# State-space mixer of a hybrid decoder layer: state products after all within-chunk products, the mask as an f32r product, transposes behind the f32r products

## The chip, the cores and the metric

The kernel runs on one core of a Trainium2 chip. The metric is the device time of one execution in microseconds, the median over repeated runs. A profile of one execution stands beside it; its times are microseconds from the first instruction unless marked ns.

## The reference, cut to what matters

One layer over 512 tokens: a normalisation, one input projection, two token mixers (a gated linear attention and a state-space mixer), one output projection, then a retrieval feed-forward over 16,384 experts and a last normalisation. The change lies in the state-space mixer, which works in four chunks of 128 tokens, with 8 heads of width 64 in 2 groups:

```python
seg = a_cum[:, :, :, None] - a_cum[:, :, None]
Lmat = jnp.exp(jnp.where(causal, seg, -jnp.inf))
Xdt = X * dt[..., None]
scores = jnp.einsum('bclgn,bcsgn->bclsg', Cm, Bm)
y_diag = jnp.einsum('bclsg,bclsgj,bcsgjp->bclgjp', scores, Lmat, Xdt)
decay_to_end = jnp.exp(a_cum[:, :, -1:] - a_cum)
states = jnp.einsum('bclgn,bclgj,bclgjp->bcgjpn', Bm, decay_to_end, Xdt)
...
y_off = jnp.einsum('bclgn,bcgjpn,bclgj->bclgjp', Cm, S_prev, jnp.exp(a_cum))
y = y_diag + y_off + X * d_skip.astype(f32).reshape(G, J)[..., None]
```

`y_diag` is the within-chunk product of a head, `y_off` its state product with the state that the earlier chunks left; the first chunk has no state.

## The kernel before

The order of work is written out by hand: each engine runs its instructions in the order in which the program issues them, and semaphores tie the engines together. One chunk `t` of the state-space mixer is three functions.

`ssd_a(t)` prepares. TensorE transposes the four blocks of X (L563, into `px`). For each of the two groups it forms the decay exponents of four heads with one f32r product each, whose operands have 40 rows (L569), adds the causal mask to all four with one product of a bf16 identity with a bf16 mask, 512 columns wide (L571), and ScalarE takes eight exponentials into `lm`. Four more f32r products with 40 rows give the decay for the state products (L578, into `ce` by VectorE). In chunks 0 to 2 one more transpose (L594) follows, then two f32 products with 64 rows, the scores (L601), which VectorE multiplies into `lm`. VectorE also scales X into `xdt` and `xdw`.

`ssd_b(t)` has, for each of the 8 heads, the within-chunk product (L614: 128 rows by 64 output partitions) and, from chunk 1 on, the state product added to it in the same PSUM region (L616: 64 rows by 64 output partitions; the row half is the group's, the output half is the head's parity). Then come the two products for the next state (L620). VectorE adds the skip term, gates, and with ScalarE's square makes `ysq`.

`ssd_c(t)` takes the group means (L647), an inverse root on ScalarE and VectorE, and splits the result into two f32r parts.

An f32 product is two instructions on TensorE, an f32r product is one. Between these functions the program places the output projection, `op(t, half, cols)`: twelve f32r products of 512 columns for each half of a token tile and of the columns (L108, L109, L110), and the residual and second normalisation (`hout_a`, `hout_b`, `n2out`; the transposes of the last are L716). PSUM has eight banks, handed out by `pt()` in turn as tiles are given back; a new tile waits for the last reader of the bank that it gets.

Of the kernel before, what the change touches and what calls it, by code (L numbers as in the profile page):

```python
# [8 lines left out]
F32R = mybir.dt.float32r  # L9
F16 = mybir.dt.float16  # L10
BF = mybir.dt.bfloat16
# [18 lines left out]
def bc(ap, axis, n):  # L30
    shape = list(ap.shape)
    shape.insert(axis, n)
    ix = tuple([slice(None)] * axis + [None])
    return ap[ix].to_broadcast(shape)
# [29 lines left out]
class Layer:  # L64
# [25 lines left out]
    def act(self, out, in_, f, **k):  # L90
        return self.S.activation(out, in_, f, **k)  # L91
# [4 lines left out]
    def tt(self, out, x, y, op):  # L96
        return self.V.tensor_tensor(out, x, y, op=op)  # L97

    def stt(self, out, x, s, y, op0, op1, **k):
        return self.V.scalar_tensor_tensor(out, x, s, y, op0=op0, op1=op1, **k)  # L100
# [31 lines left out]
    def mixers(self):  # L132
        tc, nc, a, V, T, ps = self.tc, self.nc, self.a, self.V, self.T, self.ps
        act, tt, stt, load = self.act, self.tt, self.stt, self.load
        ctx = ExitStack()
        c = ctx.enter_context(tc.tile_pool(name="mx", bufs=1))
        cr_ctx = ExitStack()
        cr = cr_ctx.enter_context(tc.tile_pool(name="mxr", bufs=1, side="right"))
        ident = self.ident

        def pt(shape=(128, 512)):
            return ps.tile(list(shape), F32, name="pm", tag="pm", bufs=8)

        def b4(dt=F32, shape=(128, 1024)):
            return c.tile(list(shape), dt, name="b4", tag="b4", bufs=29)

        def tp(shape=(128, L)):
            return cr.tile(list(shape), F32, name="tp", tag="tp", bufs=11)
# [9 lines left out]
        def ahead(i, nl=None, ns=None):  # L158
            nl, ns = look if nl is None else (nl, ns)
            while seen[0] <= min(i + nl, len(blocks) - 1):  # L160
                j = seen[0]
                raws[j] = cr.tile([128, 1024], F32, name="wraw", tag="wraw", bufs=3)
                load(raws[j], blocks[j])
                seen[0] += 1
            while seen[1] <= min(i + ns, len(blocks) - 1):
                j = seen[1]
                parts[j] = b4(F32R), b4(F32R)
                self.split(parts[j][0], parts[j][1], raws.pop(j), j < 2 or 19 <= j < 31)
                seen[1] += 1
# [93 lines left out]
        px = [pt() for _ in range(8)]  # L263
# [3 lines left out]
        for dc in range(8):  # L267
# [3 lines left out]
            stt(nl[dc], px[dc], wmix[:, dc:dc + 1], nh[dc].bitcast(F32), OP.mult, OP.subtract)  # L271
            if dc == 4:
                ahead(0, 3, 1)
        negm = c.tile([128, 128], BF, name="negm")
        identb = c.tile([128, 128], BF, name="identb")
        V.tensor_copy(negm, negm0)
        V.tensor_copy(identb, ident)

        selE, selH = c.tile([40, 4, 128], F32R, name="selE"), c.tile([40, 8], F32R, name="selH")
        V.memset(selE.bitcast(F32)[0:32], 0.0)  # L280
# [198 lines left out]
        SG, SZ, XB = [], [], {}  # L479
# [78 lines left out]

        def ssd_a(t):
            ts = slice(t * 128, (t + 1) * 128)  # L560
            px = pt()
            for b in range(4):
                T.transpose(px[:, b * 128:(b + 1) * 128], XB[b][:, ts], ident)  # L563
            lm = b4(F32, (128, 8, 128))
            for g in range(2):
                p = pt()
                for j in range(4):
                    h = 4 * g + j
                    T.matmul(p[:, j * 128:(j + 1) * 128], selH[:, h:h + 1].to_broadcast([40, 128]), acs[:, ts],  # L569
                             start=j == 0, stop=False, skip_group_check=True)  # L570
                T.matmul(p, identb, bc(negm, 1, 4), start=False, stop=True, skip_group_check=True)  # L571
                for j in range(4):
                    h = 4 * g + j
                    act(lm[:, h, :], p[:, j * 128:(j + 1) * 128], AF.Exp, bias=nacT(t)[:, h:h + 1])
            LM[t] = lm
            p = pt()
            for j in range(4):
                T.matmul(p[:, j * 128:(j + 1) * 128], selE[:, j, :], eas[:, ts], start=True, stop=True)  # L578
            ce = tp((128, 4, 128))
            p3 = p.rearrange("p (j l) -> p j l", j=4)  # L580
            tt(ce, p3, bc(XB[5][:, ts], 1, 4), OP.mult)
            de = c.tile([128, 4], F32, name="de", bufs=2)
            V.tensor_copy(de, p3[:, :, 127])
            CE[t], DEC[t] = ce, de
            px3 = px.rearrange("p (h n) -> p h n", h=8)
            xdt, xdw = tp((128, 8, 64)), None
            tt(xdt, px3, bc(dtT(t), 2, 64), OP.mult)
            if t < NT - 1:
                xdw = tp((128, 8, 64))
                tt(xdw, px3, bc(dwT(t), 2, 64), OP.mult)  # L590
            pb = None
            if t < NT - 1:
                pb = pt()
                T.transpose(pb[:, :128], XB[4][:, ts], ident)  # L594
                bt = c.tile([128, 128], F32, name="bt", bufs=2)
                act(bt, pb[:, :128], AF.Copy)
                pb = bt
            psc = [pt(), pt()]
            for g in range(2):
                r = slice(g * 64, g * 64 + 64)  # L600
                T.matmul(psc[g][:, :128], XB[4][r, ts], XB[5][r, ts], start=True, stop=True)  # L601
                tt(lm[:, 4 * g:4 * g + 4, :], lm[:, 4 * g:4 * g + 4, :], bc(psc[g][:, :128], 1, 4), OP.mult)
            XT[t] = xdt, xdw, pb

        def ssd_b(t):
            ts = slice(t * 128, (t + 1) * 128)
            xdt, xdw, bt = XT.pop(t)
            lm, ce, S = LM.pop(t), CE.pop(t), Sd[t]
            py = [pt(), pt()]
            for h in range(8):  # L610
                g, j = h // 4, h % 4
                r = slice(g * 64, g * 64 + 64)
                o = py[g][(j % 2) * 64:(j % 2) * 64 + 64, (j // 2) * 128:(j // 2) * 128 + 128]
                T.matmul(o, xdt[:, h, :], lm[:, h, :], start=True, stop=S is None)  # L614
                if S is not None:
                    T.matmul(o, S[r, j, :], ce[r, j, :], start=False, stop=True)  # L616
            if t < NT - 1:
                pst = pt()
                for g in range(2):
                    T.matmul(pst[g * 64:g * 64 + 64, :256], bt[:, g * 64:g * 64 + 64], xdw[:, 4 * g:4 * g + 4, :],  # L620
                             start=True, stop=True)
                pst3 = pst[:, :256].rearrange("p (j n) -> p j n", j=4)
                Sn = c.tile([128, 4, 64], F32, name="Sd", bufs=2)
                if S is None:
                    act(Sn, pst3, AF.Copy)
                else:
                    tt(Sn, S, bc(DEC[t], 2, 64), OP.mult)
                    tt(Sn, Sn, pst3, OP.add)
                Sd[t + 1] = Sn
            y = tp((128, 4, 128))  # L630
            for b in range(4):
                stt(y[:, b, :], XB[b][:, ts], dsk[:, b:b + 1], py[b // 2][:, (b % 2) * 128:(b % 2) * 128 + 128],
                    OP.mult, OP.add)
            for b in range(2):
                tt(y[:, 2 * b:2 * b + 2, :], y[:, 2 * b:2 * b + 2, :], sz_[b][:, :, ts], OP.mult)
            ysq = tp((128, 4, 128))
            act(ysq, y, AF.Square)
            tt(ysq[:, 0:4:2, :], ysq[:, 0:4:2, :], ysq[:, 1:4:2, :], OP.add)
            yy[t] = y, ysq
# [123 lines left out]
        flush()  # L763
        self.table("natural_log_exp_and_others")
        ssd_a(0)
        op(1,0,(1,))
        ssd_b(0)
        ssd_a(1)
        ssd_c(0)
        wo(4)  # L770
        op(0,0,(0,))
        xload(2)
        ssd_b(1)
        op(0,1,(0,))
        xload(1)
        xload(0)
        op(0,1,(1,))
        hout_a(0)
        ssd_a(2)
        hout_b(0)  # L780
        ssd_c(1)
        op(2,0,(1,))
        ssd_b(2)
        n2out(0)
        op(1,1,(0,))
# [681 lines left out]
```

## Time and profile before

| | us |
|---|---|
| median of 3 runs (lowest, highest) | 1524.52 (1524.38, 1526.88) |
| profiled execution, its own time | 1525.01 |
| its span, first to last instruction | 1523.2 |
| TensorE busy in the span | 1479.2 |
| VectorE busy | 1168.4 |
| ScalarE busy | 632.3 |
| GpSimd busy | 451.6 |

The profile is one execution. The span is 1.8 us shorter than that execution's own time, and that execution is 0.5 us above the median. The state-space chunks lie between 171.4 and 243 us of the span. Busy time counts a matmul until its modelled end, and matmuls overlap, so the distance between two starts tells more of a product's cost than its duration.

### The profile page before, as it was taken

The numbers are of one execution on the slowest core, as the hardware profiler recorded it, in microseconds if no ns is written. First come the engines' busy times: TensorE is split into PE (matmuls) and PEld (weight loads), VectorE is DVE, ScalarE is ACT, GpSimd is POOL, SyncE is SP. The second block draws the span as 40 slices with busy tenths as digits, with TensorE's granted clock in tenths as the row PEclk, the third lists the DMA queues.
The fourth block names the chain that finished last, engine by engine and source line by source line (L and its number), as shares of the span: only waits on it lengthen the run. The fifth ranks groups of instructions, "written<-read, shape, count | busy, mean of one in ns | idle before, by whom it ended". The sixth has DMA issues, their size and how long they took to land.

```text
span 1523.2 us, 22401 instructions
## 1 busy us (share of the span) xinstructions
PE 1479.2 (97%) x7904; PEld 1290.1 (85%) x7904; DVE 1168.4 (77%) x2473; ACT 632.3 (42%) x1201; POOL 451.6 (30%) x380
## 2 busy tenths in 40 slices
PE   7999999999988999989999999999999999999997
PEld 6777767888988999878999999999889998888886
DVE  6543654599999999977777777787788788888886
ACT  5335633433653544433333333333333333444444
POOL 1002403444564000002333333333243333334332
PEclk9999999999999999999999999999999999999999
DMA  5231213322334556658889888889889897888894
GB/s 186 83 125 56 70 53 131 108 84 90 105 110 140 157 150 169 180 180 301 317 304 322 317 307 303 318 309 316 297 317 316 314 322 257 293 301 301 298 327 178
DMA packets 148738, 335.56 MB, mean 220 GB/s; under 512 B 64640, under 2 KB 73872, under 8 KB 148496
## 3 DMA queue, kind: packets, MB, share of 16 engines
q1 hardware_dynamic: 58672, 186.32, 36.0%
q0 software_dynamic: 36864, 134.23, 24.6%
q10 hardware_dynamic: 53088, 13.57, 3.8%
q8 instruction: 62, 1.02, 0.3%
q14 instruction: 52, 0.43, 0.1%
HBM read 315.79 MB, written 18.28 MB: 219 GB/s over the span
## 4 chain that ended last, share of the span: by engine, by line
PE 53%; issue 20%; DVE 13%; POOL 9%; DMA 3%; ACT 2%; POOLq 0%; SPq 0%; DVEq 0%; ACTq 0%
PE pm L108 16%; PE pm L109 16%; PE pm L110 16%; POOL gat L1133 8%; DVE gat L97 4%; PE pg L1184 2%; DVE ul L104 1%; DVE B L97 1%; PE pm L902 1%; DMA gd<-stage 1%; DVE ring L97 1%; DVE eq L97 1%; DVE A L97 1%; ACT b L91 1%; DMA gat<-in_u,idx 1%
## 5 line engine op out<-in xcount | busy, mean ns | idle before, releaser
L108 PE MATMUL pm<-nT,uh 128*128 128x384 f32 (+1 forms) x1152 | 404.3, 351 | 8.6 <-ACT uh L91 8.1
L109 PE MATMUL pm<-nT,uh 128*128 128x384 f32 (+1 forms) x1152 | 399.1, 346 | 0.5 <-DVE nT L97 0.5
L110 PE MATMUL pm<-nT,ul 128*128 128x384 f32 (+1 forms) x1152 | 397.5, 345 | 1.1 <-POOL ul L104 0.9
L109 PE MATMUL pm<-vl,hh 128*128 128x512 f32 x765 | 301.5, 394 | 1.2 <-DVE vl L104 1.2
L110 PE MATMUL pm<-vh,hl 128*128 128x512 f32 x765 | 300.9, 393 | 0.0
L108 PE MATMUL pm<-vh,hh 128*128 128x512 f32 x765 | 300.6, 393 | 0.2 <-ACT vh L91 0.2
L1133 POOL DMA_INDIRECT gat<-in_u,idx x128 | 137.8, 1076 | 477.6 <-DVE gat L100 470.3
L91 ACT ACTIVATE uh<-ur 128x512 fp32r<-128x512 f32 x288 | 180.2, 629 | 219.3 <-PE pm L109 185.9
L108 PEld LDWEIGHTS pm<-nT,uh 128*128 128x128 f32 x1152 | 218.0, 189 | 34.3 <-ACT uh L91 8.6
L109 PEld LDWEIGHTS pm<-nT,uh 128*128 128x128 f32 x1152 | 217.7, 189 | 25.4 <-DVE nT L97 1.1
L110 PEld LDWEIGHTS pm<-nT,ul 128*128 128x128 f32 x1152 | 217.8, 189 | 8.7 <-POOL ul L104 2.6
L1133 POOL DMA_INDIRECT gat<-in_v,idx x128 | 148.4, 1159 | 256.1 <-DVE n2a L100 223.1
L91 ACT ACTIVATE vh<-vr 128x512 fp32r<-128x512 f32 x255 | 159.5, 626 | 136.9 <-PE pm L110 136.9
L104 DVE TENSOR_TENSOR vl<-vr,vh 128x512 fp32r<-128x512 f32 x255 | 175.2, 688 | 33.5 <-ACT vh L91 33.0
L104 DVE TENSOR_TENSOR ul<-ur,uh 128x512 fp32r<-128x512 f32 x206 | 140.7, 689 | 61.5 <-ACT uh L91 61.3
L100 DVE SCALAR_TENSOR_TENSOR n2a<-gat,dots,n2a 128x1024 f32<-128x1024 f32 x128 | 163.9, 1280 | 24.2 <-DMA gat<-in_v,idx 19.2
L110 PEld LDWEIGHTS pm<-vh,hl 128*128 128x128 f32 x765 | 143.5, 188 | 32.7 <-DVE hl L104 0.3
L100 DVE SCALAR_TENSOR_TENSOR gat<-gat,n2a 128x1024 f32<-128x1024 f32 x128 | 156.1, 1220 | 13.9 <-DMA gat<-in_u,idx 13.7
L109 PEld LDWEIGHTS pm<-vl,hh 128*128 128x128 f32 x765 | 143.9, 188 | 15.6 <-DVE vl L104 1.9
L108 PEld LDWEIGHTS pm<-vh,hh 128*128 128x128 f32 x765 | 144.0, 188 | 14.2 <-ACT vh L91 0.7
L104 POOL TENSOR_TENSOR ul<-ur,uh 128x512 fp32r<-128x512 f32 x82 | 116.5, 1427 | 101.3 <-ACT uh L91 101.2
L91 ACT ACTIVATE gl<-pm 128x384 f32<-128x384 f32 (+16 forms) x104 | 46.0, 442 | 223.8 <-PE pm L110 223.8
(254 smaller groups left out, 1709.2 us busy)
## 6 DMA issues: line engine op xcount, KB each, us to landing
ur<-in_uT SPq DMA_DIRECT2D x128, 512.0 KB, 5.9
vr<-in_v SPq DMA_DIRECT2D x128, 512.0 KB, 5.5
gd<-stage ACTq DMA_DIRECT2D x6, 2208.0 KB, 14.7
ring<-gd SPq DMA_DIRECT2D x69, 192.0 KB, 5.6
wraw<-in_w_in SPq DMA_DIRECT2D x23, 512.0 KB, 4.3
ur<-in_w_query SPq DMA_DIRECT2D x16, 512.0 KB, 3.6
b<-in_x SPq DMA_DIRECT2D x8, 512.0 KB, 3.7
wraw<-in_w_out SPq DMA_DIRECT2D x8, 512.0 KB, 3.9
```

The lines of the kernel that those rows point to most:

```text
L91: return self.S.activation(out, in_, f, **k)
L97: return self.V.tensor_tensor(out, x, y, op=op)
L100: return self.V.scalar_tensor_tensor(out, x, s, y, op0=op0, op1=op1, **k)
L104: (self.G if pool else self.V).tensor_tensor(lo, src, hi.bitcast(F32), op=OP.subtract)
L108: T.matmul(out, lhi, rhi, start=start, stop=False)
L109: T.matmul(out, lhi, rlo, start=False, stop=False)
L110: T.matmul(out, llo, rhi, start=False, stop=stop)
L902: T.matmul(p[:, t * 128:(t + 1) * 128], q[:, t * 128:(t + 1) * 128], skT[:, b, :], start=True, stop=True)
L1133: G.indirect_dma_start(out=r, out_offset=None, in_=src, in_offset=bass.IndirectOffsetOnAxis(ap=idx[:, k:k + 1], axis=0))
L1184: T.matmul(o, A[:, t // 2, :, t % 2], B[:, i, t // 2, :, t % 2], start=i == 0, stop=i == 1)
```

## The change

The within-chunk products of all eight heads of a chunk are issued first, and then the eight state products, in an order that alternates the row half and the output half; the start flag, which every within-chunk product carried before, is now set for the first product of each output half in a bank. The mask and its identity are held in f32r where they were bf16. The four transposes of X go from the head of `ssd_a` to behind the products of L578, and with them the point at which their PSUM bank is taken. No instruction is added or left out.

```diff
-        negm = c.tile([128, 128], BF, name="negm")
-        identb = c.tile([128, 128], BF, name="identb")
+        negm = c.tile([128, 128], F32R, name="negm")
+        identr = c.tile([128, 128], F32R, name="identr")
         V.tensor_copy(negm, negm0)
-        V.tensor_copy(identb, ident)
+        V.tensor_copy(identr, ident)
...
         def ssd_a(t):
             ts = slice(t * 128, (t + 1) * 128)
-            px = pt()
-            for b in range(4):
-                T.transpose(px[:, b * 128:(b + 1) * 128], XB[b][:, ts], ident)
             lm = b4(F32, (128, 8, 128))
...
-                T.matmul(p, identb, bc(negm, 1, 4), start=False, stop=True, skip_group_check=True)
+                T.matmul(p, identr, bc(negm, 1, 4), start=False, stop=True, skip_group_check=True)
...
                 T.matmul(p[:, j * 128:(j + 1) * 128], selE[:, j, :], eas[:, ts], start=True, stop=True)
+            px = pt()
+            for b in range(4):
+                T.transpose(px[:, b * 128:(b + 1) * 128], XB[b][:, ts], ident)
             ce = tp((128, 4, 128))
...
             py = [pt(), pt()]
+            out = lambda g, j: py[g][(j % 2) * 64:(j % 2) * 64 + 64, (j // 2) * 128:(j // 2) * 128 + 128]
+
             for h in range(8):
                 g, j = h // 4, h % 4
-                r = slice(g * 64, g * 64 + 64)
-                o = py[g][(j % 2) * 64:(j % 2) * 64 + 64, (j // 2) * 128:(j // 2) * 128 + 128]
-                T.matmul(o, xdt[:, h, :], lm[:, h, :], start=True, stop=S is None)
-                if S is not None:
-                    T.matmul(o, S[r, j, :], ce[r, j, :], start=False, stop=True)
+                T.matmul(out(g, j), xdt[:, h, :], lm[:, h, :], start=j < 2, stop=S is None, skip_group_check=True)
+            if S is not None:
+                for g, j in ((0, 0), (1, 1), (0, 1), (1, 0), (0, 2), (1, 3), (0, 3), (1, 2)):
+                    r = slice(g * 64, g * 64 + 64)
+                    T.matmul(out(g, j), S[r, j, :], ce[r, j, :], start=False, stop=True, skip_group_check=True)
```

## Rows read from the trace of the kernel before

**Rows 1.** Span and mean granted TensorE clock of the core.

```profile
core 0: 1523.2 us, clock 0.992
```

**Rows 2.** Busy time by stretch: engines (instructions), granted clock, DMA share, GB/s.

```profile
183.30:190.15 6.85, 6.76 (x20) 5.16 (x19) 4.70 (x12) 2.76 (x8) 0.00 (x0) 0.50 0.00 0
...
209.70:243.00 33.30, 33.30 (x177) 23.37 (x177) 16.96 (x43) 10.16 (x24) 0.55 (x1) 1.00 0.24 95
...
400.00:500.00 100.00, 89.97 (x554) 86.10 (x553) 94.54 (x136) 53.70 (x93) 52.60 (x34) 0.97 0.38 122
...
800.00:1500.00 700.00, 699.01 (x3350) 613.00 (x3349) 556.62 (x815) 266.33 (x503) 245.27 (x218) 1.00 0.88 307
```

**Rows 3.** Timeline of TensorE, 178 to 197 us: start, length, instructions (of several merged).

```profile
178.31 1.09 PE L614 MATMUL pm<-b,tp 128*64 128x128 f32 x16
...
190.44 0.43 PE L614 MATMUL pm<-b,tp 128*64 128x128 f32 x2
190.80 0.43 PE L616 MATMUL pm<-tp,Sd 64*64 64x128 f32 x2
...
196.21 0.65 PE L620 MATMUL pm<-tp,bt 128*64 128x256 f32 x4
```

**Rows 4.** Timeline of TensorE in the attention mixer, around 87 us.

```profile
86.87 0.68 PE L451 MATMUL pm<-b,ket 64*64 64x128 f32 x16
87.48 1.16 PE L465 MATMUL pm<-att,b 128*128 128x128 f32 x8
88.57 0.66 PE L474 MATMUL pm<-b,Sg 64*128 64x64 f32 x8
```

**Rows 5.** Timeline of TensorE, chunk 2's preparation.

```profile
202.14 0.39 PE L110 MATMUL pm<-b,b 128*128 128x512 f32 x1
202.38 0.60 PE L563 MATMUL pm<-ident,b 128*128 128x128 f32 x4
202.90 0.66 PE L569 MATMUL pm<-acum,selH 40*128 40x128 f32 x4
203.49 0.39 PE L571 MATMUL pm<-negm,identb 128*128 128x512 bf16 x1
203.81 0.66 PE L569 MATMUL pm<-acum,selH 40*128 40x128 f32 x4
...
205.31 0.33 PE L594 MATMUL pm<-ident,b 128*128 128x128 f32 x1
205.57 0.49 PE L601 MATMUL pm<-b 64*128 64x128 f32 x4
```

**Rows 6.** Timeline of TensorE, chunk 3's preparation.

```profile
221.20 0.66 PE L569 MATMUL pm<-acum,selH 40*128 40x128 f32 x4
...
222.11 0.66 PE L578 MATMUL pm<-ea,selE 40*128 40x128 f32 x4
222.50 0.54 PE L601 MATMUL pm<-b 64*128 64x128 f32 x4
222.97 0.50 PE L108 MATMUL pm<-b,b 128*128 128x512 f32 x1
223.31 0.40 PE L109 MATMUL pm<-b,b 128*128 128x512 f32 x1
```

**Rows 7.** The mask product's line, its weight load: ns min/median/max.

```profile
L571 PEld LDWEIGHTS <-identb x8: 95/96/97, 172.6 to 221.8; 128*128 128x128 bf16 x8
```

**Rows 8.** Waits of TensorE, 165 to 250 us: total us, times, longest.

```profile
PEld pm L108 <- ACT b L91: 0.3, 1, 0.3
PE pm L647 <- DVE de L583: 0.3, 1, 0.3
...
PEld pm L569 <- DVE nT L97: 0.2, 1, 0.2
```

**Rows 9.** Timeline of VectorE, end of chunk 2.

```profile
216.16 0.42 DVE L97 TENSOR_TENSOR Sd<-Sd,pm 128x256 f32<-128x256 f32 x1 [2.71 <-PE pm L620]
...
219.47 1.29 DVE L97 TENSOR_TENSOR nT<-pm,nT 128x512 fp32r<-128x512 f32 x2
```

## The prediction, made before the changed kernel was run

> **What bounds the kernel now.** I looked first at the span and the clock [rows 1], then at the busy time by stretch [rows 2], to see which engine has no slack where the change lies and what lies behind it. Between 209.7 and 243 us TensorE is busy for all 33.3 us, VectorE for 17.0 and ScalarE for 10.2: the stretch of the state-space chunks goes at TensorE's pace. From 800 to 1500 us TensorE is busy 699.0 of 700 us. Between 400 and 500 it is VectorE that is full (94.5 of 100), on work that TensorE's earlier results feed. The other engines and the transfers follow these two by buffers and semaphores, so what is taken out of the chunks should arrive at the end whole, unless something in the chunks takes TensorE's place. I then read TensorE's timeline in the chunks [rows 3, 5, 6], the same kind of work in the attention mixer [rows 4], and who waits for whom [rows 8].
>
> **How a switch shows.** "Busy" hides it, since matmuls overlap; distances between starts show it. In chunk 0, where no state product exists, the eight within-chunk products are 16 instructions in one block [rows 3]: the last starts at 178.31 + 1.09 - 0.27 (one instruction's length) = 179.13, so 15 steps take 0.82 us and one product costs 0.11. In chunk 1, where products with 128 and with 64 rows alternate, each costs 190.80 - 190.44 = 0.36. A switch thus adds 0.25 to every one of the 16.
>
> What makes it a switch? Two readings: the operand's height (128 rows against 64 or fewer) or its type (f32, f32r, bf16). From the last L465 (87.48 + 1.16 - 0.28 = 88.36) to the first L474 lie 0.21 us instead of 0.11 [rows 4], and both are f32; only the height changes. From the last L578 (222.11 + 0.66 - 0.27 = 222.50) to the first L601 there is no gap at all [rows 6], though f32r goes to f32: 40 rows and 64 count alike. From L110 to L563, f32r to f32 transposes of the same height, the step is 0.24 [rows 5], the usual one of 512 columns (0.23). So the height decides. The Trainium skill says the same (TensorEngine Tiling, Key Properties): changing the tiling mode, not just the tile, drains the engine. By that rule the mask edit, which leaves 128 rows between 40 and 40, removes no drain; the trace agrees, as the three steps just read show.
>
> **The regrouped products.** Before, a block with state products lasts 196.21 - 190.44 = 5.77 us, up to L620 [rows 3]. After it there are eight within-chunk products at chunk 0's pace, 0.82 us to the last start and 0.20 to the first state product (0.1 of it for the change of height): 1.02. For eight 64-by-64 products in one block there is a row: the 16 instructions of L451 take 87.48 - 86.87 = 0.61 us to the next product of another height [rows 4]; the new order also goes round the four quarters of the array. Together 1.63, so 4.14 us less for each of chunks 1 to 3: 12.4. Bounds: if only two state products run side by side, the block is 8 x 0.11 + 0.2 = 1.1 and the saving 3.7 per chunk, 11.0 in all; if each change of the row half costs a full switch, it is 8 x 0.36 = 2.9 and the saving 1.9, 5.6 in all. The upper end is 13.0, with the 0.2 of the switch hidden. I take 12.4, since L451 is the same shape and L474, which adds to finished products as here, also shows no extra wait.
>
> **The mask.** Eight products, still switched to and from. A bf16 one lasts 0.39 and the next starts 203.81 - 203.49 = 0.32 later [rows 5]. An f32r product of the same size right after a switch lasts 0.50 (L108 at 222.97), and its successor starts 0.34 later where 0.23 is usual [rows 6]: 0.11 more, because its weights are not loaded early. So 8 x 0.11 = 0.9 us lost. Between a gain of 1.5 (type were what matters: 0.09 on either side, eight times) and this loss I take the loss, whose row is nearest. The bf16 identity's load is 96 ns [rows 7]; the Trainium skill (TensorE: Matmul & The Clock Gate, weight-path perf modes) says that the fast weight load works for 128 weights of any type but f32, and gives about columns / 1.2 ns otherwise, 107 ns here and about half of that when fast. It speaks against this edit, as the rows do; by it the loss would be about 0.4 us, an estimate from that page.
>
> **The transposes.** In chunks 0 to 2 a switch on one side replaces one on the other: before, L563 follows the output projection without one, and one comes before L569 and one before L594; after, one comes before L569, one before L563, and L563 and L594 run together. The sum is zero. In chunk 3, without L594, the free step from L578 to L601 is lost: a switch before L569 (0.1), one of 0.2 before L563, 0.26 before L601 (as 205.31 to 205.57 [rows 5]), against the 0.2 saved behind L563: 0.35 lost. In exchange the exponents start some 0.3 us earlier in each chunk, and waits of 0.3 (L108 on the exponentials) and 0.3 (L647 on VectorE) [rows 8] cover part of the mask's cost in chunks 0 to 2: I count 0.5 back, at least 0, at most 0.8. The two casts keep their number and size. No DMA or queue entry moves.
>
> **What becomes late.** VectorE's adds to the state waited 2.71 us for L620 in chunk 2 [rows 9]. With TensorE 4.1 us ahead in chunk 2's preparation, 0.2 more from the moved transposes, and 4.1 more behind L616, VectorE can follow only by 4.3 + 2.7 = 7.0. The split of the normalised tokens (L97 into nT), which was at 219.47, then starts at 212.5, and its two halves of 0.65 give back two banks at 213.1 and 213.7. Chunk 3's first L569 waited on that split already [rows 8]. Taken one bank later in the order, since `px` no longer comes first, it is the second L569, at 221.20 - 8.7 = 212.5 [rows 6], that wants the first of these banks: 0.6 us of waiting. If it is still the first L569, 1.5. I take 0.6.
>
> **Sum.** 12.4 - 0.9 - 0.35 + 0.5 - 0.6 = 11.05 us; the span would be 1512.2. The profiled execution took 1525.01 with a span of 1523.2 [rows 1], and the median of the runs is 1524.52, so I set 1524.52 - 11.05 = 1513.5 us.
>
> **Rivals.**
>
> *The clock.* Between 183.3 and 190.15 us it was granted at half, 1.2 GHz of 2.4 (0.50 in [rows 2]), right behind chunk 1's preparation. If all of that stretch stretches with the clock it costs 3.4 us. The denser products could make it go away: 1510. A second stretch like it, behind the preparation of chunk 2 or 3, adds up to 3.4: 1515 to 1517. For no change: the products ahead of it, chunk 0's and chunk 1's preparation, keep their number. Chances 0.1 and 0.12.
>
> *VectorE becomes the bound of the chunks.* It is busy 17.0 us of 33.3 [rows 2]; with 8.3 taken out that is 17 of 25, and its chains with ScalarE are long. If TensorE waits for it in chunks 2 and 3 for 2 to 3 us each, or the state products run singly, 5 us of the gain go: 1518.5. Against it: the waits of [rows 8] are 0.3 us and shorter. 0.1.
>
> *The type, not the height, makes the switch.* The mask then gains 1.5 instead of losing 0.9: 1511. Against it the three steps above. 0.04.
>
> *The gain is lost behind the chunks,* as the edit does its work but the gathers or transfers set the end: 1524.5. DMA is 0.88 busy between 800 and 1500 us; against it, TensorE idles 1 us in those 700. 0.06.
>
> *Slower.* The clock stays at half through the chunks, its place being the sparse preparations. At half clock 6.85 us cost 3.4, so the gain of 11 is gone at some 22 us of such clock, and 30 us of it give 1528. Against it: only one of four preparations was followed by it. 0.03.
>
> The main case has 0.55. By itself it lies within 1511.5 and 1515.5 (the saving 11.0 to 13.0, the waits of the banks, 0.8 or 0 given back). The range takes in both clock cases, the type and half of VectorE's: 1509.5 to 1518.5. Within 0.2%, about 3 us, is what a measurement of this kernel can tell from no change. Faster: 0.91 (0.55 + 0.1 + 0.12 + 0.1 + 0.04); same 0.06; slower 0.03.
>
> **What would show it.** Right: L614 in blocks of 16 and L616 in blocks of 16, 1.6 us from the first to L620 in chunks 1 to 3; L571 at 0.50; L563 behind L578; chunk 3's L569 waiting for nT; everything after 243 us earlier by about 11. Wrong: L616 at more than 1.1 us a block; L571 closer than 0.2 to its neighbours; waits of TensorE on VectorE above 1 us in a chunk; a granted clock of 0.50 in another place; or an 11 us lead at 260 us that shrinks by 700.

## The result, and the profile of the changed kernel

| | before | changed |
|---|---|---|
| median of the first runs, us (lowest, highest) | 1524.45 (1524.38, 1526.88) | 1505.48 (1502.44, 1508.30) |
| profiled execution, us | 1525.01 | 1503.02 |
| its span, us | 1523.2 | 1501.2 |

The ratio is 0.9889, 95% interval 0.9861 to 0.9917. The change is faster, by more than was forecast: 1505.48 lies 4 us below the low end of the range. In two later sets of runs the same program gave 1513.84 us (ratio 0.9930, 0.9905 to 0.9955) and 1510.94 us (0.9926, 0.9897 to 0.9955), both inside the range. So the question is not only why the first profile is 22.0 us shorter, but why the same kernel differs by 8 us from one set of runs to another.

The span and the clock of the changed kernel, against [rows 1]:

```profile
core 0: 1501.2 us, clock 0.991
```

TensorE's timeline in the changed kernel: chunk 0's first products, chunk 1's products, the way from the last product ahead of chunk 2's preparation to chunk 2's products, and chunk 3's preparation (start, length, instructions):

```profile
178.46 1.09 PE L614 MATMUL pm<-b,tp 128*64 128x128 f32 x16
...
187.56 1.09 PE L614 MATMUL pm<-b,tp 128*64 128x128 f32 x16
188.59 0.67 PE L618 MATMUL pm<-tp,Sd 64*64 64x128 f32 x16
189.19 0.65 PE L622 MATMUL pm<-tp,bt 128*64 128x256 f32 x4
...
195.17 0.39 PE L110 MATMUL pm<-b,b 128*128 128x512 f32 x1
...
204.16 1.09 PE L614 MATMUL pm<-b,tp 128*64 128x128 f32 x16
...
209.81 0.39 PE L110 MATMUL pm<-b,b 128*128 128x512 f32 x1
210.13 0.66 PE L566 MATMUL pm<-acum,selH 40*128 40x128 f32 x4
210.72 0.50 PE L568 MATMUL pm<-negm,identr 128*128 128x512 f32 x1
211.15 0.66 PE L566 MATMUL pm<-acum,selH 40*128 40x128 f32 x4
211.74 0.50 PE L568 MATMUL pm<-negm,identr 128*128 128x512 f32 x1
212.17 0.66 PE L575 MATMUL pm<-ea,selE 40*128 40x128 f32 x4
212.76 0.66 PE L578 MATMUL pm<-ident,b 128*128 128x128 f32 x4
213.35 0.49 PE L601 MATMUL pm<-b 64*128 64x128 f32 x4
213.77 0.50 PE L108 MATMUL pm<-b,b 128*128 128x512 f32 x1
```

The last product ahead of chunk 3's preparation in the kernel before:

```profile
219.52 0.40 PE L110 MATMUL pm<-b,b 128*128 128x512 f32 x1
```

The mask's weight load in the changed kernel, against [rows 7] (ns min/median/max):

```profile
L568 PEld LDWEIGHTS pm<-negm,identr x8: 186/186/186, 172.4 to 211.7; 128*128 128x128 f32 x8
```

The line numbers moved with the edit: the state product L616 is L618 here, the update L620 is L622, the exponent products L569 are L566, the mask L571 is L568, L578 is L575, and the transposes L563 are L578. From the first L614 to L622 the block lasts 189.19 - 187.56 = 1.63 us, where [rows 3] had 5.77. The state products are one block of 16 and take 0.60 us to the next operation. In the preparation the mask lasts 0.50 and the next product starts 211.15 - 210.72 = 0.43 behind it (0.32 in [rows 5]). From the last product ahead of it to L108 the preparation takes 213.77 - 209.81 = 3.96 us; in the kernel before it takes 222.97 [rows 6] less 219.52, which is 3.45, so it grew by 0.51. No row of these products carries a wait.

VectorE's timeline in the changed kernel, the split that gives the two banks back [rows 9]:

```profile
210.31 1.29 DVE L97 TENSOR_TENSOR nT<-pm,nT 128x512 fp32r<-128x512 f32 x2
```

Busy time by stretch in the changed kernel: chunk 1's place of the half clock in [rows 2], its own half-clock stretch, and the long products behind the chunks in two parts:

```profile
183.30:190.15 6.85, 6.82 (x58) 4.91 (x58) 5.11 (x14) 2.92 (x8) 0.00 (x0) 1.00 0.22 71
...
198.27:201.68 3.41, 3.41 (x15) 2.76 (x15) 3.23 (x7) 1.86 (x7) 0.01 (x1) 0.50 0.05 18
...
718.00:981.30 263.30, 263.30 (x1331) 238.31 (x1330) 208.20 (x357) 98.79 (x192) 88.66 (x84) 1.00 0.89 315
981.30:1244.60 263.30, 263.30 (x1331) 238.31 (x1330) 212.12 (x305) 98.56 (x191) 90.46 (x83) 1.00 0.89 316
```

The same view of the kernel before, over the same products, and TensorE's one wait among them:

```profile
731.00:998.00 267.00, 267.00 (x1330) 240.69 (x1330) 208.22 (x357) 98.86 (x192) 89.21 (x84) 1.00 0.88 311
998.00:1265.00 267.00, 266.01 (x1324) 239.31 (x1322) 210.31 (x303) 97.31 (x189) 90.67 (x83) 1.00 0.88 309
```

```profile
1104.08 0.50 PE L109 MATMUL pm<-vl,hh 128*128 128x512 f32 x1 [0.98 <-DVE vl L104]
```

This is the surprise. In both programs TensorE is busy for the whole stretch at the full granted clock, with some 1,330 instructions of the same shapes; before takes 267.0 us for them, the changed kernel 263.3. Nothing in the diff touches these products. The work beside them is alike too: VectorE is busy for 208.22 and 208.20 us, and the DMA share is 0.88 and 0.89.

**Where 22.0 us went.** I compared the starts of the same TensorE instruction in both traces. At 243 us, behind the chunks, the changed kernel leads by 13.38 us; at 688 us by 12.24; at 1272 us by 21.99, and this stays to the end.

Two things must be taken out of the first lead. The first is what the execution brought along: at the last product ahead of chunk 0 (L110, at 171.30 us before and 171.47 in the changed kernel) the changed kernel was 0.17 behind. So I use the *passage*, the time from that product to the one at 243.20 us of the kernel before: 71.90 us before, 58.35 in the changed kernel.

The second is the clock: before ran 6.83 us of the chunks at half clock, the changed kernel 3.41. What this costs can be read from the changed kernel at both clocks. From the last L110 ahead of chunk 2's preparation to chunk 2's first L614 it took 204.16 - 195.17 = 8.99 us with 3.41 us at half clock, and 7.44 in a later profile without (`after_again` below, 198.47 to 205.91): 1.55. From the first L614 of chunk 0 to that of chunk 1 it took 9.10 here, and 12.12 in a later profile with 6.83 us at half clock (`head_order` below): 3.0. So:

- 0.17 was lost ahead of the chunks.
- the clock in the chunks: 3.0 - 1.55 = 1.45.
- the edits themselves: 71.90 - 58.35 - 1.45 = 12.1 us. This is an estimate, good to some 0.3 us, since 3.0 was measured in the changed kernel and is used for the kernel before.
- between 243 and 690 us 1.1 is given back. As much is lost near 400 us, where TensorE waits for GpSimd's `ul`, 0.45 and 1.60 us in the changed kernel, 0.74 in the kernel before; what comes and goes behind it cancels.
- from 690 to 1272 us, 9.75 is gained: about 1.45 at the wait of 0.98 us at 1104 us, which the changed kernel doesn't have, and 8.3 by the pace of identical products.

### The profile page after: what moved, and what is told of

It reads as the page before. It is cut to its first block, busy times and chain, and to the rows that moved or that the text cites. A ratio compares the mean times of both kernels' runs of the same rounds, so it can differ in the third digit from the quotient of the medians.

```text
span 1501.2 us, 22402 instructions
## 1 busy us (share of the span) xinstructions
PE 1456.2 (97%) x7904; PEld 1278.0 (85%) x7904; DVE 1169.4 (78%) x2473; ACT 632.7 (42%) x1201; POOL 451.7 (30%) x380
## 4 chain that ended last, share of the span: by engine, by line
PE 80%; DVE 12%; issue 3%; DMA 2%; ACT 2%; POOL 0%; SPq 0%; DVEq 0%; POOLq 0%; ACTq 0%
PE pm L109 25%; PE pm L108 25%; PE pm L110 25%; DVE gat L97 4%; PE pg L1186 2%; DVE B L97 1%; DVE ul L104 1%; PE pm L904 1%; DMA gd<-stage 1%; DVE ring L97 1%; DMA ur<-in_uT 1%; DVE eq L97 1%; DVE A L97 1%; ACT b L91 0%; ACT tp L91 0%
## 5 line engine op out<-in xcount | busy, mean ns | idle before, releaser
L108 PE MATMUL pm<-nT,uh 128*128 128x384 f32 (+1 forms) x1152 | 402.1, 349 | 8.8 <-ACT uh L91 8.3
L110 PE MATMUL pm<-nT,ul 128*128 128x384 f32 (+1 forms) x1152 | 397.0, 345 | 2.0 <-POOL ul L104 2.0
L109 PE MATMUL pm<-nT,uh 128*128 128x384 f32 (+1 forms) x1152 | 397.0, 345 | 0.5 <-DVE nT L97 0.5
L109 PE MATMUL pm<-vl,hh 128*128 128x512 f32 x765 | 300.4, 393 | 0.2 <-DVE vl L104 0.2
L110 PE MATMUL pm<-vh,hl 128*128 128x512 f32 x765 | 300.3, 393 | 0.0
L108 PE MATMUL pm<-vh,hh 128*128 128x512 f32 x765 | 299.0, 391 | 0.2 <-ACT vh L91 0.2
L108 PEld LDWEIGHTS pm<-nT,uh 128*128 128x128 f32 x1152 | 218.1, 189 | 33.5 <-ACT uh L91 8.7
L109 PEld LDWEIGHTS pm<-nT,uh 128*128 128x128 f32 x1152 | 218.1, 189 | 25.0 <-DVE nT L97 1.1
L110 PEld LDWEIGHTS pm<-nT,ul 128*128 128x128 f32 x1152 | 217.7, 189 | 9.1 <-POOL ul L104 2.9
L110 PEld LDWEIGHTS pm<-vh,hl 128*128 128x128 f32 x765 | 143.7, 188 | 30.9
L108 PEld LDWEIGHTS pm<-vh,hh 128*128 128x128 f32 x765 | 144.0, 188 | 14.2 <-ACT vh L91 0.7
L109 PEld LDWEIGHTS pm<-vl,hh 128*128 128x128 f32 x765 | 144.0, 188 | 14.1 <-DVE vl L104 0.5
```

The costliest lines, as they stand in the source:

```text
L108: T.matmul(out, lhi, rhi, start=start, stop=False)
L109: T.matmul(out, lhi, rlo, start=False, stop=False)
L110: T.matmul(out, llo, rhi, start=False, stop=stop)
```

## The experiments

Kernels that ran in one set share a chip and its runs of the kernel before. Two theories stood against each other. The pace is a state of the execution, which either kernel can be in; or it follows from the change (earlier arrival, other transfers beside it). Some kernels add products that nobody uses; none leaves out part of the computation.

To place each profile I measured, in its trace, the time from the 31st to the 221st product `pm<-vh,hh` (about 720 to 990 us). In all 18 profiles it takes one of two values, 267.09 or 263.29 us; I call them the slow and the quick pace.

**Both kernels once more,** unchanged.

> The changed kernel, unchanged. In the first trace 13.4 us of the 22 were won by 243 us, 1.2 were given back by 690, and 9.8 came between 690 and 1280 us, where the program is the same as before to the last operand and bank, and TensorE went 1.6% quicker with no waits. Theory A (a state of the execution, set at its start or at the stop near 680 us and kept): another profile of the same program can show either pace, about 1.213 or 1.233 us for six products (three of 512 and three of 384 columns), and the times fall into groups some 5 to 10 us apart. Theory B (the program sets the pace, through the place of its instructions): the pace is 1.213 in every profile, and the times scatter by 1 to 2 us round 1503.

> The kernel before, unchanged, for a second profile of it. Theory A: the pace between 690 and 1275 us can be 1.213 us for six products in some executions, with a time of about 1514; Theory B: 1.233 in every profile and 1524 to 1527 us in every run.

The changed kernel: 1513.84 us (1509.20 to 1514.62), ratio 0.9930 (0.9905 to 0.9955); before: 1524.16 (1516.31 to 1527.78). The profile of before has the slow pace. The passage of the changed kernel is 59.85 us, with as much half clock in the chunks as before (two stretches of 3.41), so without any help of the clock the edits give 12.05. It has the quick pace, and loses it. Busy time by stretch of this run, and the wait:

```profile
1080.00:1090.09 10.09, 7.37 (x37) 6.18 (x36) 4.77 (x8) 3.94 (x9) 1.86 (x2) 1.00 0.67 246
1090.09:1093.50 3.41, 3.41 (x11) 2.82 (x10) 3.41 (x5) 0.84 (x2) 1.62 (x1) 0.50 0.96 292
1093.50:1103.50 10.00, 10.00 (x52) 9.07 (x51) 8.41 (x12) 3.60 (x7) 4.68 (x4) 1.00 0.98 356
```

```profile
1088.65 0.49 PE L109 MATMUL pm<-vl,hh 128*128 128x512 f32 x1 [2.72 <-DVE vl L104]
```

TensorE waits there for VectorE (2.72 us before an L109), the clock falls for 3.41 us, and from then on the products go at the slow pace. The pace is thus not a property of the changed kernel: it left the quick pace within one execution. That the time, 1513.84, lies beside the forecast 1513.5 is therefore in part luck.

**Regrouping alone; the changed kernel with the mask in bf16.**

`regroup_only` is the kernel before with only the two loops over heads of the change. `bf16_mask` is the changed kernel with the two mask tiles back in bf16:

```diff
...
-                T.matmul(p, identr, bc(negm, 1, 4), start=False, stop=True, skip_group_check=True)
+                T.matmul(p, identb, bc(negm, 1, 4), start=False, stop=True, skip_group_check=True)
```

> Only the products regrouped; the mask stays bf16 and the transposes stay at the head. By the terms of the prediction each of chunks 1 to 3 is 4.14 us shorter from the first L614 to L620 or its successor, 12.4 in all, and the lead at 260 us is 12.4 plus or minus a low clock stretch (up to 3). With the pace of before the time is 1510 to 1513; with the pace of the changed kernel 1501 to 1504. Theory B says 1.233, since the mask's separate weight loads are still there; theory A says either.

> The changed kernel with the mask back in bf16; regrouping and moved transposes stay. The mask's term says that each f32r mask product costs 0.11 us more, 0.9 in all, of which some 0.4 is covered: so 0.4 to 0.9 us less by 260 us than in the changed kernel at the same clock. If the type of the operand made the switch, it would be 1.5 us more instead. Pace: theory A either, theory B 1.233, since the program's instruction count is back to before's.

Regrouping alone gave 1512.64 us (1510.51 to 1514.11), ratio 0.9925 (0.9901 to 0.9949). Its passage is 58.17 us with 3.41 us of half clock, so 71.90 - 58.17 - 1.45 = 12.3 by the edit; its pace is slow. With the bf16 mask: 1511.49 (1500.79 to 1514.04), ratio 0.9904 (0.9872 to 0.9936); passage 59.29 with 6.83 us of half clock, so 12.6; pace slow in the profile. The timeline of that kernel, one mask product, and behind it the same place of the changed kernel:

```profile
173.21 0.39 PE L568 MATMUL pm<-negm,identb 128*128 128x512 bf16 x1
173.53 0.66 PE L566 MATMUL pm<-acum,selH 40*128 40x128 f32 x4
```

```profile
172.37 0.50 PE L568 MATMUL pm<-negm,identr 128*128 128x512 f32 x1
172.81 0.66 PE L566 MATMUL pm<-acum,selH 40*128 40x128 f32 x4
```

The step is 0.32 in bf16 and 0.44 in f32r. That is the mask edit's local price, 0.9 for eight products. With the other two edits in place some 0.55 of it shows in the passage (59.29 against 59.85, and against 59.84 in `head_order` below, all with 6.83 us of half clock).

**The mask alone; the transposes alone.**

`mask_only` is the kernel before with the mask and its identity in f32r. `transposes_only` is the kernel before with `px` and its four transposes moved as in the change.

> Only the mask in f32r. By the prediction's term 0.11 us lost at each of eight products, 0.9 in all, less what is covered by waits: 0.4 to 0.9 later at 260 us at the same clock. If the type of the operand made the switch, 1.5 us earlier. Either is below what the time can tell; the profile decides by the distance from one L569 block to the next.

> Only the four transposes moved behind the products of L578's line. By the prediction's term: nothing in chunks 0 to 2 (one switch for another), 0.35 us lost in chunk 3, and up to 0.3 us a chunk back where exponentials start earlier: between -0.6 and +0.4 us by 260 us, at the same clock; no difference in the time that a measurement can tell. If the transposes' place decides whether the clock falls near 183 us, up to 3 us less.

The mask alone: 1526.37 us (1517.86 to 1528.51), ratio 1.0011 (0.9988 to 1.0034). The transposes alone: 1521.94 (1516.24 to 1524.12), ratio 0.9991 (0.9971 to 1.0011). Neither can be told from no change by its time. By the passage the mask takes 74.17 us, but with more half clock than the profile of before. Busy time by stretch in the kernel with the mask alone:

```profile
175.90:179.30 3.40, 3.40 (x9) 2.65 (x9) 2.20 (x4) 0.00 (x0) 0.00 (x0) 0.50 0.02 5
186.20:189.60 3.40, 3.40 (x11) 2.82 (x12) 2.38 (x6) 1.73 (x4) 0.00 (x0) 0.50 0.00 0
206.65:210.05 3.40, 3.25 (x13) 2.60 (x12) 3.40 (x7) 2.22 (x7) 0.00 (x0) 0.50 0.00 0
```

Three stretches at half clock (0.50), 10.2 us in all, where the profile of before had one of 6.85 [rows 2]. Three later profiles, of kernels whose chunks are those of before (`fill_before`, `busy_before` and `cover_before` below), have three such stretches at the same places, and passages of 73.60, 73.59 and 73.29 us: so the mask alone costs 0.6 to 0.9. The passage with the transposes alone is 70.31 with 3.41 us of half clock, so they gain 71.90 - 70.31 - 1.45 = 0.1.

Where these small amounts arise shows in each chunk's own stretch, from the last L110 ahead of its preparation to its first L614, in profiles in which it ran at the full clock (us, from the timelines; chunk 1's and the mask alone's others had half clock):

| | before | mask alone | transposes alone | changed, mask in bf16 | changed |
|---|---|---|---|---|---|
| chunk 0 | 7.00 | | 6.81 | 6.81 | 6.99 |
| chunk 2 | 7.54 | | 7.36 | 7.34 | 7.44 |
| chunk 3 | 9.57 | 9.82 | 9.86 | 9.86 | 10.07 |

The moved transposes gain 0.2 each in chunks 0 and 2, where the waits of 0.3 of L108 and L647 [rows 8] no longer stand in the trace, and lose 0.3 in chunk 3. The mask costs 0.1 to 0.2 in each of these chunks, next to the other edits too.

The kernel with the moved transposes alone, which has no regrouping, ran at the quick pace. So this pace does not need the regrouping.

**The order of the state products.**

```diff
-                for g, j in ((0, 0), (1, 1), (0, 1), (1, 0), (0, 2), (1, 3), (0, 3), (1, 2)):
+                for g, j in [(h // 4, h % 4) for h in range(8)]:
```

> The changed kernel with the state products in the order of the heads, so that four in a row share a row half. The prediction took the block of eight at 0.61 us from L451, whose order is also by row half, with the output halves alternating. If the quarters have queues of their own, the block stays at 0.6 us; if order matters, four products with only two output halves run two by two: 1.1 us a block, 1.5 us more in all.

TensorE's timeline of that run, chunks 0 and 1:

```profile
178.47 1.09 PE L614 MATMUL pm<-b,tp 128*64 128x128 f32 x16
...
190.59 1.09 PE L614 MATMUL pm<-b,tp 128*64 128x128 f32 x16
191.62 0.68 PE L618 MATMUL pm<-tp,Sd 64*64 64x128 f32 x16
192.23 0.65 PE L622 MATMUL pm<-tp,bt 128*64 128x256 f32 x4
```

1.64 us against 1.63: the alternation between the quarters of the array is worth nothing here, a block of one height is. The time is 1509.87 us (1503.88 to 1515.73), ratio 0.9910 (0.9880 to 0.9941). Its pace was slow to 1092 us and quick behind a wait of 1.03 us there, without any fall of the clock:

```profile
820.00:1080.00 260.00, 260.00 (x1296) 234.40 (x1295) 203.64 (x348) 96.06 (x186) 87.84 (x81) 1.00 0.89 314
1130.00:1240.00 110.00, 110.00 (x557) 99.65 (x556) 89.65 (x117) 41.66 (x80) 37.76 (x35) 1.00 0.90 323
```

```profile
1092.92 0.49 PE L109 MATMUL pm<-vl,hh 128*128 128x512 f32 x1 [1.03 <-DVE vl L104]
```

**Products into the long stop, first two tries.** Before the long stretch TensorE stands for more than 8 us (near 675 us, for ScalarE's `uh`) and its clock falls. If the pace is drawn there, filling the stop should fix it. Some 50 unused products went into it, half into one bank, half into another. The `busy` kernels have this edit; the `fill` kernels put 25 products into each of two new tiles of `pt()` instead.

```diff
                 vgrp(0, i)
+                if e == i == 0:
+                    for w in (pv[0][1], pv[1][1]):
+                        for _ in range(23):
+                            T.matmul(w[:, :TD], nh[0][:, :128], nh[0][:, tsd], start=True, stop=True)
```

> The changed kernel with 50 more f32r products of 384 columns (their results are not used) where TensorE waits some 8 us near 670 us for a block of expert weights. Six profiles so far: the pace of TensorE behind that wait was 1.213 us for six products in two executions (both of the changed kernel) and 1.233 in four, and it changed within one execution, at a rise of the clock. Theory A (the pace is drawn when the clock rises while products run, and kept): with TensorE busy through the wait the clock does not fall, nothing is drawn there, and the pace behind is the same in every execution and in both filled kernels. The times then scatter by 2 us or less. Theory B (the place of the instructions): the pace stays at random or as before. Either way the clock's low stretch of 7 to 10 us goes, worth up to 3 us.

> The kernel before with the same 50 products. Theory A: the same pace as the filled changed kernel, and a difference between the two of what the chunks alone give: 10.5 to 13.5 us. If the quicker pace belongs to the change, the difference is 20 us.

> The changed kernel with 46 more f32r products of 384 columns (8.0 us, results overwritten) in the wait of 8.7 us near 670 us, this time into PSUM banks that nobody reads before, so that they need wait for nothing. In ten profiles the same products behind that wait took 267.09 us (seven times) or 263.29 us (three: two of the changed kernel, one of the kernel with the transposes alone moved). Theory A (the pace is drawn at a rise of the clock): the clock does not fall near 670 us, so there is no rise, and the pace comes out the same in this and the next kernel; the 12 times lie within 4 us. Saved besides: up to half of 7 to 10 us of low clock, less 0.5 for what the products overrun. If the clock has no part in it, both paces still occur.

> The kernel before with the same 46 products. Theory A: the same pace as in the changed kernel with them, and 11 to 14 us more time, what the chunks give. If the quicker pace came with the change, 20 us.

These failed as fills. The timeline of `fill_after`:

```profile
668.39 4.52 PE L1352 MATMUL pm<-nT 128*128 128x384 f32 x25
...
677.59 6.17 PE L1352 MATMUL pm<-nT 128*128 128x384 f32 x25 [4.69 <-ACT gl L91]
```

The second half's bank was not free; it waited 4.69 us for ScalarE, the clock still fell, and the second half then ran in the way of real work. `fill_after` 1517.92 us, `busy_after` 1517.18, `fill_before` 1531.16, `busy_before` 1530.82: the kernel before lost 6.0 and 6.8 us by them, the changed one 6.2 on the chip where both were run. What follows from them is that, with both kernels treated alike, before and changed differ by 13.2 and 13.6 us, and that all four profiles have the slow pace.

**The long stop filled from one bank.** As above, with 50 products into `pv[0][1]` alone.

> The changed kernel with 50 unused products of 384 columns put in the wait of TensorE for ScalarE near 670 us, all into one accumulator bank that the products behind them overwrite; they leave out nothing of the computation. 50 x 0.173 us = 8.7 us of a wait of 9 to 10 us, so no new wait if they all go into that one bank. Theory (the pace of the long product stretch from 690 us is set when TensorE stops for long and its clock falls near 670 us): the granted clock stays full from 660 to 700 us, the half-clock spell of 3.4 to 6.8 us that stands there otherwise is gone (1.7 to 3.4 us gained), and since nothing stops there any more all executions show one pace, so that their times lie within 4 us of each other, around 1507 us or 1516 us. Rival (the pace is changed elsewhere too, at short waits and at other rises of the clock): the clock stays full at 670 us as well, but the executions still spread over 8 us or more, about 1500 to 1513 us. In both, the difference to the kernel before with the same products stays 10 to 14 us.

> The kernel before with the same 50 unused products in the wait near 670 us, all into one accumulator bank; nothing of the computation is left out. Theory (pace set at the stop near 670 us): clock full from 670 to 710 us, 1.7 to 3.4 us gained, executions within 4 us of each other, around 1521 us (or 1512 us if the pace that is kept is the quick one). Rival (pace changed elsewhere too): the same gain, executions spread over 8 us or more, about 1513 to 1526 us. In both it lies 10 to 14 us above the changed kernel with the same products.

The timeline of `cover_after`, and its busy time around the stop:

```profile
666.75 8.85 PE L1351 MATMUL pm<-nT 128*128 128x384 f32 x50
676.25 0.44 PE L108 MATMUL pm<-nT,uh 128*128 128x384 f32 x1 [0.65 <-ACT gl L91]
```

```profile
660.00:670.00 10.00, 10.00 (x58) 9.87 (x58) 3.19 (x6) 2.42 (x5) 0.43 (x1) 1.00 0.85 218
670.00:680.00 10.00, 9.35 (x52) 8.77 (x51) 4.58 (x8) 3.10 (x7) 0.89 (x1) 1.00 0.98 374
680.00:690.00 10.00, 10.00 (x52) 8.94 (x51) 6.87 (x12) 4.14 (x8) 2.35 (x3) 1.00 0.79 251
```

Now the stop is 0.65 us and the clock stays at 1.00. The lead over before falls from 12.85 to 11.64 us as the spare products run over, and then grows to 13.50, since before ran this place at half clock. Both profiles have the slow pace. The changed kernel took 1510.56 us (1504.69 to 1513.94), ratio 0.9917 (0.9885 to 0.9949); before with the products 1523.68 (1521.46 to 1525.58), ratio 1.0004 (0.9986 to 1.0021); difference 13.1. The spread of the twelve executions of before is 4.1 us, where the 17 of the plain kernel in the same set went from 1515.65 to 1527.69: the theory's figure. The six of the changed kernel spread over 9.3 us, one of them, at 1504.69, 5.9 below the median: the rival's figure. That left it open.

**The same in two more versions:** the transposes alone, and the changed kernel with the bf16 mask.

> The kernel before with the moved transposes alone, and the 50 unused products in TensorE's stop near 670 us; nothing of the computation is left out. Without the products this kernel ran 1516.2 to 1524.1 us and its profile showed the quick pace. Theory (the quick pace can be picked up only at the long stop near 670 us): the profile shows the slow pace (267.1 us for the stretch that takes 263.3 at the quick one) and all executions lie within 5 us of each other, around 1523 us, none below 1519.5. Rival (the pace does not depend on that stop): two or three of twelve executions lie at 1514 to 1518 us.

> The changed kernel with the mask product left in bf16, and the 50 unused products in TensorE's stop near 670 us; nothing of the computation is left out. Theory (the quick pace can be picked up only at the long stop near 670 us): slow pace in the profile, executions within 6 us of each other, around 1509.5 us (the f32r mask's 0.9 us below the changed kernel with the same products), none below 1505. Rival (the pace does not depend on that stop): a quarter of the executions at 1500 to 1504 us, the rest near 1509.

`cover_transp`: 1521.02 us (1515.06 to 1524.34), ratio 0.9993 (0.9973 to 1.0014). `cover_bf16`: 1509.72 us (1509.45 to 1511.79), ratio 0.9918 (0.9893 to 0.9944); its executions lie within 2.3 us, where the same kernel without the products, on another chip, spread over 13.2. Both profiles have the slow pace behind the filled stop. But `cover_transp` doesn't keep it, and two of its twelve executions lie at 1515.06 and 1515.41, as the rival had said. Its busy time on either side of its one wait in the stretch, and that wait:

```profile
820.00:1087.00 267.00, 267.00 (x1331) 240.65 (x1330) 208.57 (x357) 97.96 (x190) 89.39 (x84) 1.00 0.88 311
1130.00:1240.00 110.00, 110.00 (x557) 99.55 (x556) 89.09 (x116) 41.40 (x80) 38.20 (x35) 1.00 0.90 319
```

```profile
1100.93 0.50 PE L109 MATMUL pm<-vl,hh 128*128 128x512 f32 x1 [0.40 <-DVE vl L104]
```

267.00 / 1331 = 0.2006 us for each instruction ahead of the wait, 110.00 / 557 = 0.1975 behind it, at the full clock on both sides; the changed kernel's first profile, quick throughout, has 263.30 / 1331 = 0.1978. So the stop near 675 us is not the only place where the pace can change; the pace changed at a wait of 0.40 us. That part of the theory falls.

Unchanged kernel once more, in the set with `head_order`:

> The changed kernel once more, beside the kernel before, for the share of executions at either pace. Theory A: its times fall into groups, round 1503 to 1506 and round 1510 to 1515, and those of the kernel before round 1516 to 1519 and round 1523 to 1529; the medians differ by 11 to 13 us where both sit in the same group.

1510.94 us (1503.96 to 1514.55); the profiled execution, 1503.96, has the quick pace throughout and leads by 13.36 at 243 us (passage 58.31, with 3.41 us of half clock).

**What all 18 profiles say together.** Ten have the full stop near 675 us: four of them run at the quick pace behind it (the changed kernel three times, the transposes alone), six at the slow one (before twice, regrouping alone, the bf16 mask, the head order, the mask alone). Eight have products in that stop: all slow behind it. Nine profiles have one more wait of TensorE in the stretch, near 1085 to 1111 us (0.2 to 2.9 us beyond the usual steps): at it three change their pace (two from slow to quick, one from quick to slow) and six keep it. Nowhere in the 18 does it change while TensorE runs on. What decides which pace follows a stop isn't shown.

## Why the prediction was right in its terms and wrong in its range

**The regrouped products: right.** 1.63 us a block was forecast and 1.63, 1.62 and 1.63 (219.88 to 221.51 us) were measured in chunks 1 to 3. Regrouping alone gave 12.3 against 12.4. That height and not type makes the switch also held: the mask in f32r between operands of 40 rows gained nothing. The Trainium skill (TensorEngine Tiling, Key Properties) says that a change of tiling mode drains the engine; these blocks agree, with 14 changes fewer a chunk (16 before, 2 after) and 4.14 us gone.

**The mask: right.** 0.11 to 0.12 a product, as forecast; of these 0.9 between 0.6 and 0.9 showed in the passage with the mask alone, and some 0.55 next to the other edits. The Trainium skill (TensorE: Matmul & The Clock Gate, LDWEIGHTS and weight-path perf modes) was the source of an estimate of half of that, from a load of 107 ns and of half that when fast. The traces differ: the bf16 identity's load took 96 ns [rows 7] and the f32r one's 186, and the step grew from 0.32 to 0.43 and 0.44.

**The transposes: right.** Chunk 3's preparation grew by 0.51 with both edits (0.35, and 0.22 for two masks, were forecast), by 0.29 from L110 to L108 with the transposes alone. The 0.5 given back was nearly met too: 0.2 each in chunks 0 and 2, by the transposes alone.

**The wait for nT's banks: did not come.** 0.6 was forecast. The split started 9.16 us earlier (219.47 to 210.31): some 1.45 of it is the clock, which leaves 7.7 where 7.0 was allowed. The second product of the exponents came 10.05 earlier (221.20 to 211.15), 8.6 without the clock, where 8.7 was allowed. So the first bank came free at 210.31 + 0.65 = 210.96, before 211.15, and the step of 0.43 from the mask to that product is the one of chunk 0 (0.44). With this term gone, 11.05 becomes 11.65; 12.1 is the estimate from the profiles.

**The clock: a rival that came in part.** The stretch at 183.3 us was gone in the first profile, and another of half its length stood at 198.27 us. In the others such stretches lie between 175 and 206 us, once, twice, three times or (in `cover_transp`) not at all, and they differ from one execution to the next of one program. But they are not the same in both programs either. Up to 640 us the filled kernels are the kernels they were made from, so there are five profiles of the chunks of before, with 6.83, 6.83, 10.24, 10.24 and 10.24 us at half clock, and six of the changed kernel's, twice with 3.41 and four times with 6.83. The mean is 3.2 us lower in the changed kernel, worth some 1.4 us by the 1.55 above (6.83 us cost 3.0, where the prediction had 3.4). That rival had a chance of 0.1 and the forecast took no change; eleven executions suggest that the change brings part of it, and do not show it. VectorE, the next rival, did not become the bound: no wait of TensorE for it in the first profile's chunks is longer than 0.3 us.

**The step that failed** is the sentence that what is taken out of the chunks "should arrive at the end whole", with 1524.52 less the sum as the time. It takes the rest of the program to cost the same in both. The rest has two paces, 1.4% apart over 190 products and their neighbours, worth 8.3 us over 690 to 1272 us, and the three runs of before shown, within 2.5 us of each other, held no sign of it: later runs of before reached from 1513.91 to 1529.28. So the 3 us that the prediction held to be enough to tell a change were not. The range had terms for the chunks, and none for a spread of what lies behind them. At the slow pace the first profile would have been 1503.02 + 8.3 = 1511.3 us, inside the range and 0.2 below the main case's own. Only one of the first four executions was profiled; that the other three also owe their times to the pace isn't shown.

What stays open: what sets the pace at a stop, and whether the changed kernel meets the quick one more often. Its three profiles all began with it, but three other versions with the regrouping did not. The paired differences where the profiles have the slow pace, 13.1 to 13.6 us, need no such help: the edits' 12.1 and the clock's 1.4 make some 13.5.

## What to carry to other kernels

Products of different operand heights are cheaper in blocks than in turn: read the price from the starts of neighbours (0.36 against 0.11 us here), not from busy time, and count each change of height. Before a few microseconds of a 1.5 ms kernel are given to an edit, compare the same instructions far behind the edit in both traces: a lead that goes on growing where both programs are identical is not the edit's. Count the lead from the last common product ahead of the edit (the profiles already differed there by up to 1.0 us, as much as two of these three edits are worth), and take out what ran at another clock. A stop can be filled with spare products only from a bank that is free for its whole length; one that was not free cost 6 us and more.

## What the runs showed of the hardware that was not expected

- The same f32r products at the full granted clock ran at one of two paces, 267.09 or 263.29 us for the stretch that was measured, kept for hundreds of us. Within the stretch it changed only where TensorE had waited: behind 2.72 us with a fall of the clock, and behind 1.03 and 0.40 us without one.
- The half-clock stretches in the chunks change from execution to execution of one program: 6.83 or 10.24 us in five profiles of the chunks of before, 3.41 or 6.83 in six of the changed kernel's, at places from 175 to 207 us. 3.41 us of them cost 1.55 us.
- Eight 64-by-64 f32 state products took 0.60 and 0.61 us in the two orders, so the block's uniform height is what matters, not the round through the quarters.
